# The low parts of the second layer's input on GpSimd, and two weight splits in other places

## The chip, the cores and the metric

One core of one Trainium2 chip runs the whole kernel. The metric is the device time of one execution in microseconds (us); the kernel before took 276.52 us, the median of three runs from 276.19 to 276.76. Engines: PE (TensorE, with weight loads shown apart as PEld), DVE (VectorE), ACT (ScalarE), POOL (GpSimd), and SP, which issues the DMAs.

## The reference, cut to what matters

One step of a decoder with two layers, on 256 prompt rows and 8 sample rows (264 columns in the kernel, which keeps features on partitions). Layer 0 is a gated short convolution, layer 1 block-sparse attention:

```python
xp = layernorm(DN_ALPHA * xp + yp, ln_g[0], ln_b[0])   # end of layer 0
q, k, v, z = jnp.split(x @ w_in_attn, 4, axis=-1)      # layer 1: 32 slabs of 128 columns
```

All arithmetic is float32.

## The kernel before, in words

To multiply in float32 precision, every operand is split into a rounded high part and a low part that is the rest (low = value - high), and a product is three matmuls: high x high, low x high, high x low. Weights come in 80 slabs of 128 output columns (1024 rows, so 128 x 1024 elements in a tile). For each slab n, `load(n)` issues the DMA of `raw`, `hi(n)` rounds it on ACT (L124), `lo(n)` subtracts on DVE (L129), and `mm` sends 24 matmuls to PE (L136 to L138), 8 blocks of the contraction times three. Here "split" means `lo(n)`.

The engines' queues are written out by hand: nothing reorders them. The order comes from hooks: `at(n, phase, f, ...)` puts work into slab n, and `begin(n)` runs the phases in the order dma, pe, s0, hi, lo, s1a, s1b, s1, s1c, then hi3 and lo3, ahead of the slab's matmuls. The tables `hi_slot` and `lo_slot` say at which slab the rounding and the split of a later slab stand. The load of the slab that takes over the `raw` buffer (there are four) stands behind the split.

Slabs 40 to 47 are the q part of layer 1's input projection. The normalised input x1 isn't ready when slab 40 is due, so slabs 40 to 46 (`i < NU`) multiply the not yet normalised rows (`m0`), and the evacuation repairs it: `u_evac` copies two columns (L580), then combines acc in PSUM with the norm's rows `nr` (L582) and multiplies (L583), on DVE; `u_fin` finishes on ACT (L586), and POOL copies the sample columns to `qs` (L587). Beside this, for each of 8 blocks m, x1 itself is made:

- `x1_norm(m)`: two DVE instructions on xf (L839, L840), from `nr`;
- `x1_affine(m)`: ACT scales and shifts (L844) and rounds to the high part `m1h` (L845);
- `x1_low(m)`: DVE subtracts to the low part `m1l` (L848).

Slab 47 is the first to multiply x1. It also has in its middle, between blocks 3 and 4, the 64 matmuls of the sample rows' scores (L745), which read `zq`, filled on DVE (L736) from `qs`. PSUM has three `acc` buffers in rotation: slab 47 takes the one of slab 44, which `u_evac` of slab 44 must have read.

Of the kernel before, what the change touches and what calls it, by code (L numbers as in the profile page):

```python
# [10 lines left out]
F32 = mybir.dt.float32  # L11
# [4 lines left out]
ALU = mybir.AluOpType  # L16
# [5 lines left out]
N = T + B  # L22
# [27 lines left out]
def build(tc, a):  # L50
    nc = tc.nc
    pe, act, dve, pool, sp = nc.tensor, nc.scalar, nc.vector, nc.gpsimd, nc.sync

    with ExitStack() as top:
# [35 lines left out]
        xf = cp.tile([128, NB, N], F32, name="xf")  # L90
# [40 lines left out]
        def mm(acc, n, mv, ks, first=True, last=True):  # L131
            mh, ml = mv
            w = acc.shape[-1]
            for k in ks:
                wh, wl = his[n][:, k, :], los[n][:, k, :]
                pe.matmul(acc, wh, mh[:, k, 0:w], start=first and k == ks[0], stop=False)  # L136
                pe.matmul(acc, wl, mh[:, k, 0:w], start=False, stop=False)  # L137
                pe.matmul(acc, wh, ml[:, k, 0:w], start=False, stop=last and k == ks[-1])  # L138
# [4 lines left out]
        def at(n, phase, f, *args):  # L143
            hooks.setdefault((n, phase), []).append(lambda: f(*args))

        def run(n, phase):
            for f in hooks.pop((n, phase), []):
# [2 lines left out]
        hi_slot = {4: 3, 5: 3, 6: 3, 7: 4, 8: 4, 9: 5, 10: 5, 11: 6, 38: 33, 39: 34, 40: 22, 41: 24, 42: 26,  # L150
                   43: 36, 44: 37, 45: 40, 46: 41, 47: 43, 48: 45, 49: 46, 50: 47, 51: 48, 52: 48, 53: 49,
                   54: 51, 55: 52, 56: 53, 57: 53, 58: 54, 65: 61, 66: 62, 67: 63, 68: 63, 78: 74}
        lo_slot = {4: 3, 5: 3, 6: 3, 7: 4, 8: 5, 9: 5, 45: 40, 46: 42, 47: 44, 51: 49, 52: 49,
                   53: 50, 54: 51, 55: 52, 56: 53, 57: 54, 58: 54, 61: 58, 62: 59, 63: 60, 64: 61, 65: 61, 66: 62, 67: 63, 39: 34}

        order = []
# [4 lines left out]
        for i, n in enumerate(order):  # L161
            hs = hi_slot.get(n, n - 5)
            late = "3" if 45 <= n < 50 else ""
            at(hs, "hi" + late, hi, n)
            ls = lo_slot.get(n, hs + 1)
            if n in (61, 62, 65):
                late = "4"
            elif ls in (56, 57, 58):
                late = "3"
            elif n == 46:  # L170
                late = ""
            at(ls, "lo" + late, lo, n)
            if i + 4 < len(order):
                at(ls, "lo" + late, load, order[i + 4])
# [360 lines left out]
        with tc.tile_pool(name="l1", bufs=1) as p1, ExitStack() as late_pool:  # L535
            x1 = pair[1]
# [305 lines left out]
            def x1_affine(m):  # L842
                c = xf[:, m]
                act.activation(c, c, AF.Identity, bias=ln.bcol(m), scale=ln.gcol(m))  # L844
                act.copy(x1[0][:, m, 0:N], c)  # L845

            def x1_low(m):
                dve.tensor_sub(x1[1][:, m, 0:N], xf[:, m], x1[0].bitcast(F32)[:, m, 0:N])  # L848

            S = 40  # L850

# [34 lines left out]
            for h in range(8):  # L886
                n = S + 16 + h
# [155 lines left out]
            split_late(41)  # L1043
            for m in (0, 1):
                x1_affine(m)
            mm(ac2[1], 41, pair[0], range(3, 7), first=False, last=False)
            for i in range(2):
                mm(ac2[i], 40 + i, pair[0], range(7, 8), first=False)
                at(42, "s0", u_evac, i, ac2[i])
                at(42, "s1", u_fin, i)  # L1050
            for n, norm, low in ((42, (2, 3), ()), (43, (4, 5), (0, 1)), (44, (6, 7), ()),
                                 (45, (), (2, 3)), (46, (), (4, 5, 6, 7))):
                for m in norm:
                    at(n, "s1", x1_norm, m)
                    at(n, "s1", x1_affine, m)
                for m in low:
                    at(n, "s1", x1_low, m)
            for i in range(2, 32):
                n = S + i
# [159 lines left out]
```

## Time and profile before

| what | value |
|---|---|
| median of 3 runs | 276.52 us (276.19 to 276.76) |
| the profiled execution | 276.77 us, of which the profile's span 275.0 us |
| busy | PE 98%, DVE 74%, ACT 62%, POOL 24% of the span |
| granted clock of PE | 1.00 |
| chain that ended last | PE 98% |

The span goes from the first to the last instruction; 1.8 us of the execution lie outside of it. A row of the order of time gives start, duration, engine, line, operation, output and inputs with shape; idle time of the engine ahead of it and what ended it stand in brackets. Matmuls overlap, so the distance of their starts tells more than their durations, and on the other engines, too, an instruction can start shortly before the last one has ended.

### The profile page before, as it was taken

The numbers are of one execution on the slowest core, as the hardware profiler recorded it, in microseconds if no ns is written. First come the engines' busy times: TensorE is split into PE (matmuls) and PEld (weight loads), VectorE is DVE, ScalarE is ACT, GpSimd is POOL, SyncE is SP. The second block draws the span as 40 slices with busy tenths as digits, with TensorE's granted clock in tenths as the row PEclk, the third lists the DMA queues.
The fourth block names the chain that finished last, engine by engine and source line by source line (L and its number), as shares of the span: only waits on it lengthen the run. The fifth ranks groups of instructions, "written<-read, shape, count | busy, mean of one in ns | idle before, by whom it ended". The sixth has DMA issues, their size and how long they took to land.

```text
span 275.0 us, 6282 instructions
## 1 busy us (share of the span) xinstructions
PE 270.2 (98%) x2307; PEld 254.7 (93%) x2307; DVE 203.5 (74%) x415; ACT 170.6 (62%) x348; POOL 64.9 (24%) x129
## 2 busy tenths in 40 slices
PE   8999999999999999999999999999999999999994
PEld 5999999999999999999999997999959996998883
DVE  3888966655775857979999839799857484994745
ACT  4786554453655628549686665888746854599302
POOL 1121532020110101961312365721100030000122
PEclk9999999999999999999999999999999999999999
DMA  7976879999785875142223999997989955782012
GB/s 245 401 274 223 281 286 333 396 360 377 245 266 197 283 227 189 56 147 76 80 76 99 343 401 357 337 393 233 354 308 348 391 183 174 219 272 75 1 76 88
DMA packets 24336, 66.48 MB, mean 242 GB/s; under 512 B 3058, under 2 KB 6898, under 8 KB 24178
## 3 DMA queue, kind: packets, MB, share of 16 engines
q1 hardware_dynamic: 23874, 65.69, 68.0%
q8 instruction: 18, 0.29, 0.4%
q10 hardware_dynamic: 432, 0.39, 0.4%
q14 instruction: 12, 0.10, 0.1%
HBM read 61.67 MB, written 3.35 MB: 236 GB/s over the span
## 4 chain that ended last, share of the span: by engine, by line
PE 98%; ACT 0%; DVE 0%; issue 0%
PE acc L136 24%; PE acc L137 24%; PE acc L138 24%; PE c L1010 4%; PE acc L472 3%; PE sd L745 3%; PE dps L796 3%; PE c1b L1010 2%; PE acc L1010 2%; PE acc L475 1%; PE so L1123 1%; PE warmp L80 1%; PE s L679 1%; PE o L717 1%; PE pt L707 1%; PE s L677 1%
## 5 line engine op out<-in xcount | busy, mean ns | idle before, releaser
L124 ACT CAST hi<-raw 128x1024 fp32r<-128x1024 f32 x76 | 79.0, 1049 | 34.3 <-DMA raw<-w 15.7
L129 DVE TENSOR_TENSOR lo<-raw,hi 128x1024 fp32r<-128x1024 f32 x76 | 92.7, 1230 | 7.1 <-ACT hi L124 3.9
L136 PE MATMUL acc<-m0h,hi 128*128 128x264 f32 (+1 forms) x280 | 79.4, 283 | 0.0
L138 PE MATMUL acc<-m0l,hi 128*128 128x264 f32 (+1 forms) x280 | 79.2, 283 | 0.0
L137 PE MATMUL acc<-m0h,lo 128*128 128x264 f32 (+1 forms) x280 | 79.2, 283 | 0.0
L136 PE MATMUL acc<-m1h,hi 128*128 128x264 f32 x264 | 76.4, 289 | 0.0
L138 PE MATMUL acc<-m1l,hi 128*128 128x264 f32 x264 | 74.6, 282 | 0.0
L137 PE MATMUL acc<-m1h,lo 128*128 128x264 f32 x264 | 74.5, 282 | 0.0
L137 PEld LDWEIGHTS acc<-m0h,lo 128*128 128x128 f32 x280 | 52.8, 189 | 0.0
L136 PEld LDWEIGHTS acc<-m0h,hi 128*128 128x128 f32 x280 | 52.6, 188 | 0.1
L138 PEld LDWEIGHTS acc<-m0l,hi 128*128 128x128 f32 x280 | 52.7, 188 | 0.0
L136 PEld LDWEIGHTS acc<-m1h,hi 128*128 128x128 f32 x264 | 49.6, 188 | 1.7 <-issue 0.8
L137 PEld LDWEIGHTS acc<-m1h,lo 128*128 128x128 f32 x264 | 49.8, 189 | 0.0
L138 PEld LDWEIGHTS acc<-m1l,hi 128*128 128x128 f32 x264 | 49.5, 188 | 0.0
L428 POOL COPY uo<-up 128x10 f32<-128x10 f32 x8 | 9.0, 1122 | 64.3 <-DVE up L427 58.5
L635 POOL COPY vs<-vh 128x8 f32<-128x8 f32 x8 | 3.0, 375 | 33.1 <-ACT vh L634 33.1
L688 DVE CUSTOM_DVE_ANT_0 P<-s,cst 128x128 f32<-128x128 f32 (+1 forms) x16 | 5.1, 355 | 6.2 <-PE s L679 6.2
L436 DVE SCALAR_TENSOR_TENSOR t<-up,cst,t 128x256 f32<-128x256 f32 x8 | 3.9, 483 | 6.9 <-ACT t L435 6.9
L825 POOL COPY zs<-z 128x8 f32<-128x8 f32 x8 | 3.0, 378 | 24.4 <-ACT z L824 24.4
L824 ACT ACTIVATE z<-acc 128x264 f32<-128x264 f32 x8 | 3.1, 386 | 9.0 <-PE acc L138 9.0
L952 ACT ACTIVATE zq<-raw 128x1024 f32<-128x1024 f32 x8 | 8.5, 1061 | 0.1
L427 DVE TENSOR_TENSOR up<-acc,h 128x264 f32<-128x264 f32 x8 | 3.4, 430 | 6.9 <-PE acc L138 6.9
(226 smaller groups left out, 446.5 us busy)
## 6 DMA issues: line engine op xcount, KB each, us to landing
raw<-w SPq DMA_DIRECT2D x76, 512.0 KB, 4.5
kv<-kc SPq DMA_DIRECT2D x32, 256.0 KB, 6.2
kv<-vc SPq DMA_DIRECT2D x16, 512.0 KB, 6.4
first<-first SPq DMA_DIRECT2D x6, 388.0 KB, 7.1
v_o<-vh SPq DMA_DIRECT2D x8, 132.0 KB, 5.5
xf<-kall SPq DMA_DIRECT2D x16, 64.0 KB, 2.6
kall<-gb SPq DMA_DIRECT2D x1, 1024.0 KB, 6.1
k_o<-kall SPq DMA_DIRECT2D x6, 132.0 KB, 5.4
```

Of the source, the lines that this page charges most:

```text
L124: act.copy(his[n][sl], raws[n][sl])
L129: dve.tensor_sub(los[n][sl], raws[n][sl], his[n].bitcast(F32)[sl])
L136: pe.matmul(acc, wh, mh[:, k, 0:w], start=first and k == ks[0], stop=False)
L137: pe.matmul(acc, wl, mh[:, k, 0:w], start=False, stop=False)
L138: pe.matmul(acc, wh, ml[:, k, 0:w], start=False, stop=last and k == ks[-1])
L428: pool.tensor_copy(uo[:, f], up[:, T:N + 2])
L472: pe.matmul(accs[s], wh, (mh, ml)[c], start=k == 0 and c == 0, stop=False)
L688: dve.tensor_tensor_reduce(out=P[sl], in0=s_ps[h][sl], in1=mask[sl], scale=-SCALE, scalar=3e38, op0=ALU.add, op1=ALU.min, accum_out=mx[:, ...
L745: pe.matmul(s[32 * j:32 * j + 16, 0:256], zq[:, o:o + 16], kt, start=step == 0 and i == 0, stop=step == 3 and i == 3)
L796: pe.matmul(dps[0][32 * j:32 * j + 32, 512 * c:512 * c + 512], pm[b2][pg][:, j, :], kv_tiles[step, j][:, 512 * c:512 * c + 512], start=ste ...
L952: act.activation(od, wide(raws, k), AF.Copy, accum_out=wsum[:, k:k + 1])
L1010: pe.matmul(acc, g[m][:, k, t], wide(d, k)[:, c0:c1], start=k == 0 and i == 0, stop=k == 7 and i == 2)
```

## The change

Three things are moved. All eight `x1_low` go from DVE to POOL, each pair behind its `x1_affine`. The splits of slabs 45 and 46 each stand one place later on DVE, behind evacuations. And the affines of blocks 6 and 7 stand behind `u_fin` of slab 43 on ACT.

```diff
-        lo_slot = {... 45: 40, 46: 42, 47: 44, ...}
+        lo_slot = {... 45: 42, 46: 43, 47: 44, ...}
...
-            elif n == 46:
+            elif n in (45, 46):
                 late = ""
...
             def x1_low(m):
-                dve.tensor_sub(x1[1][:, m, 0:N], xf[:, m], x1[0].bitcast(F32)[:, m, 0:N])
+                pool.tensor_tensor(x1[1][:, m, 0:N], xf[:, m], x1[0].bitcast(F32)[:, m, 0:N], ALU.subtract)
...
             for m in (0, 1):
                 x1_affine(m)
+                x1_low(m)
...
-            for n, norm, low in ((42, (2, 3), ()), (43, (4, 5), (0, 1)), (44, (6, 7), ()),
-                                 (45, (), (2, 3)), (46, (), (4, 5, 6, 7))):
+            for n, norm, low in ((42, (2, 3), ()), (43, (4, 5), (2, 3)), (44, (6, 7), (4, 5)),
+                                 (45, (), (6, 7))):
                 for m in norm:
                     at(n, "s1", x1_norm, m)
-                    at(n, "s1", x1_affine, m)
+                    at(n, "s1c" if n == 44 else "s1", x1_affine, m)
```

On POOL, from the copies of `nr` to the copy of `qs` of the fourth slab (q3); `zq`, `pr` and `pm` are cleared there. Before:

```order
L357 COPY nr_1903<-st0_1896 32x132 x4
L587 COPY qs_1862<-q0_1853 128x8
L587 COPY qs_1862<-q1_1854 128x8
L566 MEMSET zq_2027 128x1160
...
L587 COPY qs_1862<-q2_1855 128x8
L587 COPY qs_1862<-q3_1856 128x8
```

After:

```order
L357 COPY nr_1903<-st0_1896 32x132 x4
L848 TENSOR_TENSOR m1l_92<-xf_87,m1h_91 128x264 x2
L587 COPY qs_1862<-q0_1853 128x8
L587 COPY qs_1862<-q1_1854 128x8
L566 MEMSET zq_2025 128x1160
...
L848 TENSOR_TENSOR m1l_92<-xf_87,m1h_91 128x264 x2
L587 COPY qs_1862<-q2_1855 128x8
L848 TENSOR_TENSOR m1l_92<-xf_87,m1h_91 128x264 x2
L587 COPY qs_1862<-q3_1856 128x8
```

Low parts 4 and 5 now stand behind the copy of q2, and the copy of q3 behind them.

On DVE, from slab 41's evacuation (acc_1873) over slab 42's (t2_2038 before, t2_2036 after) to the norms that follow. Before:

```order
L583 TENSOR_TENSOR t2_1979<-t2_1979,nr_1903 128x264
L129 TENSOR_TENSOR lo46_1982<-raw46_1620,hi46_1948 128x1024
L839 TENSOR_TENSOR xf_87<-xf_87,nr_1903 128x264
...
L583 TENSOR_TENSOR t2_2038<-t2_2038,nr_1903 128x264
...
L848 TENSOR_TENSOR m1l_92<-xf_87,m1h_91 128x264 x2
L580 COPY uv_2086<-acc_2061 128x2
```

After:

```order
L583 TENSOR_TENSOR t2_1977<-t2_1977,nr_1903 128x264
L129 TENSOR_TENSOR lo45_1980<-raw45_1616,hi45_1913 128x1024
L839 TENSOR_TENSOR xf_87<-xf_87,nr_1903 128x264
...
L583 TENSOR_TENSOR t2_2036<-t2_2036,nr_1903 128x264
L129 TENSOR_TENSOR lo46_2039<-raw46_1620,hi46_1944 128x1024
...
L580 COPY uv_2088<-acc_2063 128x2
```

Split 45, which stood ahead of the first norms, takes the place of split 46; split 46 stands behind slab 42's evacuation, and the low parts are gone from ahead of slab 43's evacuation (L580).

On DVE, from slab 47's split over slab 44's evacuation to the filling of `zq`. Before:

```order
L129 TENSOR_TENSOR lo47_2103<-raw47_1743,hi47_2059 128x1024
L580 COPY uv_2132<-acc_2107 128x2
L582 SCALAR_TENSOR_TENSOR t2_2134<-nr_1903,uv_2132,acc_2107 128x264
L583 TENSOR_TENSOR t2_2134<-t2_2134,nr_1903 128x264
L848 TENSOR_TENSOR m1l_92<-xf_87,m1h_91 128x264 x2
L622 STREAM_SHUFFLE qsr_2168<-qs_1862 32x32
```

After:

```order
L129 TENSOR_TENSOR lo47_2107<-raw47_1743,hi47_2061 128x1024
L580 COPY uv_2136<-acc_2111 128x2
L582 SCALAR_TENSOR_TENSOR t2_2138<-nr_1903,uv_2136,acc_2111 128x264
L583 TENSOR_TENSOR t2_2138<-t2_2138,nr_1903 128x264
L622 STREAM_SHUFFLE qsr_2172<-qs_1862 32x32
```

The order of split and evacuation is the same; two low parts are gone behind them.

More of the change, by code (lines that the diff above doesn't have):

```diff
@@ L152, in build @@
                    54: 51, 55: 52, 56: 53, 57: 53, 58: 54, 65: 61, 66: 62, 67: 63, 68: 63, 78: 74}
-        lo_slot = {4: 3, 5: 3, 6: 3, 7: 4, 8: 5, 9: 5, 45: 40, 46: 42, 47: 44, 51: 49, 52: 49,
+        lo_slot = {4: 3, 5: 3, 6: 3, 7: 4, 8: 5, 9: 5, 45: 42, 46: 43, 47: 44, 51: 49, 52: 49,
                    53: 50, 54: 51, 55: 52, 56: 53, 57: 54, 58: 54, 61: 58, 62: 59, 63: 60, 64: 61, 65: 61, 66: 62, 67: 63, 39: 34}
```

## The prediction

> **What bounds the kernel now.** I read the page first (busy shares, chain), then PE's own waits, then the order of time on PE, DVE, ACT and POOL between 114 and 150 us, where the change lies.
>
> ```profile
> span 275.0 us, 6282 instructions
> PE 270.2 (98%) x2307; PEld 254.7 (93%) x2307; DVE 203.5 (74%) x415; ACT 170.6 (62%) x348; POOL 64.9 (24%) x129
> ...
> PE 98%; ACT 0%; DVE 0%; issue 0%
> ...
> raw<-w SPq DMA_DIRECT2D x76, 512.0 KB, 4.5
> ```
>
> The chain is PE nearly throughout. All idle time of PE that the trace puts down to somebody:
>
> ```profile
> PE warmp L80 <- PEq L1200: 0.8, 1, 0.8
> PE st L1139 <- ACT zq L1136: 0.5, 1, 0.5
> PE sd L745 <- issue: 0.2, 1, 0.2
> ```
>
> Only the last line, 0.2 us, lies where the change is. So the change can win hardly anything directly: work taken off DVE shortens the time only if PE waits for DVE. It can lose, if something that PE needs comes late. Where is that closest? At the start of slab 47, the first that reads x1 (columns: start us, us, engine, line):
>
> ```profile
> 142.11 0.28 PE L136 MATMUL acc<-m1h,hi 128*128 128x264 f32 x1
> ...
> 143.43 0.28 PE L138 MATMUL acc<-m1l,hi 128*128 128x264 f32 x1
> 143.86 0.50 PE L745 MATMUL sd<-kv,zq 128*16 128x256 f32 x2 [0.16 <-issue]
> ```
>
> The same stretch on DVE, before:
>
> ```profile
> 127.09 0.43 DVE L839 TENSOR_TENSOR xf<-xf,nr 128x264 f32<-128x264 f32 x1
> 127.56 0.44 DVE L840 TENSOR_TENSOR xf<-xf,nr 128x264 f32<-128x264 f32 x1
> ...
> 128.72 0.15 DVE L580 COPY uv<-acc 128x2 f32<-128x2 f32 x1
> ...
> 129.43 0.43 DVE L583 TENSOR_TENSOR t<-t,nr 128x264 f32<-128x264 f32 x1
> ...
> 130.84 1.22 DVE L129 TENSOR_TENSOR lo<-raw,hi 128x1024 fp32r<-128x1024 f32 x1
> 131.98 0.42 DVE L839 TENSOR_TENSOR xf<-xf,nr 128x264 f32<-128x264 f32 x1
> ...
> 134.38 0.43 DVE L583 TENSOR_TENSOR t<-t,nr 128x264 f32<-128x264 f32 x1
> 134.73 0.43 DVE L839 TENSOR_TENSOR xf<-xf,nr 128x264 f32<-128x264 f32 x1
> ...
> 136.35 0.77 DVE L848 TENSOR_TENSOR m1l<-xf,m1h 128x264 fp32r<-128x264 f32 x2
> 137.04 0.15 DVE L580 COPY uv<-acc 128x2 f32<-128x2 f32 x1
> ...
> 139.82 1.22 DVE L129 TENSOR_TENSOR lo<-raw,hi 128x1024 fp32r<-128x1024 f32 x1
> 140.96 0.15 DVE L580 COPY uv<-acc 128x2 f32<-128x2 f32 x1
> 141.15 0.49 DVE L582 SCALAR_TENSOR_TENSOR t<-nr,uv,acc 128x264 f32<-128x264 f32 x1
> ...
> 143.47 0.27 DVE L736 COPY zq<-qs 128x16 f32<-128x16 f32 x2
> ```
>
> DVE runs back to back. There are three acc buffers, so slab 47 writes into slab 44's, which L582 reads until 141.15 + 0.49 = 141.64. From a DVE end to the matmul that it frees takes 0.12 us (zq ends at 143.47 + 0.27 = 143.74, L745 starts at 143.86). PE could have started slab 47 at 141.76 and did at 142.11: **the spare is 0.35 us**. Whatever makes DVE later than that there, PE loses, and nothing gives it back, since PE has no idle time after it that could shrink.
>
> **Part 1: order and work of DVE.** What the norms wait for ahead of 127.09, on ACT:
>
> ```profile
> 124.78 2.17 ACT L357 COPY nr<-st 32x132 f32<-32x132 f32 x7
> ```
>
> A split (lo) costs DVE 131.98 - 130.84 = 1.14 us; two low parts 137.04 - 136.35 = 0.69. Before, slab 45's split ran ahead of 127.09, where DVE would otherwise have waited for ACT's copies of nr. Those end at 124.78 + 2.17 = 126.95; with the split gone the norms start at about 127.03, 0.06 earlier. Between there and 141.64 stand now both splits (45 takes 46's place, 46 comes behind the next evacuation: +1.14) and two low parts less (-0.69). Together -0.06 + 1.14 - 0.69 = +0.39. Against the spare of 0.35 that alone is 0.04 us of stall.
>
> **Part 2: eight low parts on POOL.** No row shows this operation there. The nearest is POOL's addition of the same shape, also with two SBUF inputs:
>
> ```profile
> 114.58 1.61 POOL L328 TENSOR_TENSOR sr<-sr,xf 128x264 f32<-128x264 f32 x1 [0.55 <-DVE xf L300]
> 116.15 0.95 POOL L329 TENSOR_TENSOR q<-q,sqm 128x264 f32<-128x264 f32 x1
> ...
> 120.50 0.76 POOL L329 TENSOR_TENSOR q<-q,sqm 128x264 f32<-128x264 f32 x1
> ```
>
> 0.76 us alone, 0.95 to 1.61 beside these rows of DVE:
>
> ```profile
> 114.36 1.21 DVE L129 TENSOR_TENSOR lo<-raw,hi 128x1024 fp32r<-128x1024 f32 x1
> 115.49 0.99 DVE L510 SCALAR_TENSOR_TENSOR m0l<-xf,cst,m0h 128x264 fp32r<-128x264 f32 x1
> 116.40 0.42 DVE L313 SCALAR_TENSOR_TENSOR xf<-ln,xf 128x264 f32<-128x264 f32 x1
> ```
> ```profile
> L510 DVE SCALAR_TENSOR_TENSOR m0l<-xf,cst,m0h 128x264 fp32r<-128x264 f32 x2 | 0.9, 488 | 0.0
> ```
>
> These exclude each other. POOL's row of 114.58 ends at 116.19, 0.62 after the split beside it (115.57): it worked only from 0.14 before the split's end. L510, 0.49 alone, then took 0.99 and ended at 116.48, 0.29 after POOL: it worked only from 0.20 before POOL's end. L313, with one input from PSUM, took its 0.42 in the middle of POOL's row: unhindered. So DVE's rows with two SBUF inputs (L129, L583, L839, L840) exclude a low part on POOL; L580 and L582, which read acc in PSUM, don't. In a dense row of DVE, the next instruction would start 0.08 before the last one's end e (114.36 + 1.21 - 115.49); with POOL in between it starts at e - 0.14 + 0.76 - 0.20 = e + 0.42. **A low part on POOL costs DVE up to 0.50 us, against 0.345 on DVE itself**, and nothing where it falls beside L580 and L582 or idle time: bounds 0 and 0.50 each. Which it is follows from when each rounding (m1h, L845) is out on ACT:
>
> ```profile
> 128.67 0.41 ACT L845 CAST m1h<-xf 128x264 fp32r<-128x264 f32 x1
> ...
> 129.63 0.41 ACT L845 CAST m1h<-xf 128x264 fp32r<-128x264 f32 x1
> ...
> 133.55 0.41 ACT L845 CAST m1h<-xf 128x264 fp32r<-128x264 f32 x1
> ...
> 134.50 0.41 ACT L845 CAST m1h<-xf 128x264 fp32r<-128x264 f32 x1
> ...
> 137.57 0.51 ACT L586 ACTIVATE q<-t,uv 128x264 f32<-128x264 f32 x1
> ...
> 145.31 1.98 ACT L124 CAST hi<-raw 128x1024 fp32r<-128x1024 f32 x2
> ```
>
> POOL follows ACT by 0.07 us (L586 above ends at 138.08):
>
> ```profile
> 138.15 0.19 POOL L587 COPY qs<-q 128x8 f32<-128x8 f32 x1 [4.30 <-ACT q L586]
> ```
>
> - Low 0: rounding out at 129.08, so on POOL from 129.15. L583 of the first evacuation, due at 129.37, starts at 129.15 + 0.76 - 0.20 = 129.71: 0.34.
> - Low 1: rounding out at 130.04, on POOL until 130.87, beside L580 and L582 of the second evacuation: 0.
> - Low 2: everything is 0.34 - 0.06 = 0.28 later by now. Rounding out at 133.96 + 0.28, on POOL from 134.31; L583, due at 134.66, starts at 134.87: 0.21.
> - Low 3: rounding out at 134.91 + 0.28 = 135.2, just as slab 46's split begins. It runs behind the split and pushes the next L839: 0.50.
> - Lows 4 and 5 stand in POOL's queue behind the copy of qs, which waits for L586, which stands behind the affines on ACT. These are 0.28 + 0.21 + 1.14 + 0.50 = 2.13 later now, so L586 ends at 140.2. Low 4 then gets in between the last L839 and its L840. Such an L840 would start 0.04 behind its L839 (127.09 + 0.43, 127.56), and now 0.42: 0.38. Low 5 follows at once, ahead of slab 47's split: 0.50.
>
> Sum of waits: 0.34 + 0.21 + 0.50 + 0.38 + 0.50 = 1.93. With part 1, L582 ends 2.32 late, at 143.96, and slab 47 starts at 144.08 instead of 142.11: **stall 2.0 us**.
>
> By the Trainium skill (SBUF — State Buffer, section "Who interferes with whom") a DVE instruction with two SBUF inputs contends with a GpSimd instruction that reads SBUF, and the second to issue is blocked until the first has finished. The trace agrees in kind; by the word of the rule DVE would wait to the full end of POOL's row, 0.20 longer than L510 did, and the estimate with five such waits would be 3.0 us of stall instead of 2.0.
>
> **Covered parts.** Lows 6 and 7 are needed in slab 47's second half, behind the 64 L745, whose time hides them:
>
> ```profile
> L745 PE MATMUL sd<-kv,zq 128*16 128x256 f32 x64 | 4.0, 379 | 0.2 <-issue 0.2
> ```
>
> Without that cover they would be a few tenths late, as they end near 145. Splits 45 and 46 end near 130.84 + 1.22 + 0.28 = 132.3 and, begun at 135.2, 136.4; their slabs start two and one slab ahead of 47, and a slab is 24 matmuls of (143.43 - 142.11) / 11 = 0.12 us, 2.9: at 136.3 and 139.2. That hides 46 by 2.7 us. On SP the loads of slabs 49 and 50 wait for those splits and start some 4 to 5 us later; nothing of SP stands behind them in that time that is due, and with 4.5 us to land they arrive by 141, ahead of the roundings of 49 and 50 at 145.31. The affines of 6 and 7 move behind one L586 on ACT: only lows 6 and 7 follow. The zq copies lose four low parts ahead of them (-1.39) but inherit the waits, so they end near 145.4 for L745 due 0.2 behind 144.08 + 143.43 - 142.11 = 145.4: the 0.2 us that PE waited there before may go or stay. I take 0.
>
> Sum: +2.0 on the profiled execution's 276.77, so 278.8; that run was 0.25 above the median, which gives **278.5** against 276.52.
>
> **Rivals.**
> - Not slower: POOL's low parts fall beside PSUM readers or cost DVE nothing, as beside L313. Then part 1 alone stands, 0.0 to 0.2 of stall, and the 0.2 at L745 may go: 276.3 to 276.7. It decides if the waits sum to under 0.5 us (0.55 for 0.2% less the 0.04). Against it: L510 twice its length. For it: L313.
> - Half: POOL's queue meets only two or three dense places, because DVE's next instruction gets in first. Stall 0.4 to 1.4: 276.9 to 277.9.
> - More: every one of the six low parts ahead of 47 costs the full 0.50, or DVE waits for POOL's full row: 6 x 0.50 + 0.04 = 3.0, 279.5. Against it: the 0.20 by which L510 worked ahead of POOL's end, and low 1's place.
>
> **How the numbers follow.** This measurement tells about 0.2% (0.55 us) from no change. Forecast (stall 1.4 to 2.6, so 277.9 to 279.1): 0.62. More: 0.06. Half: 0.14, of which 0.04 ends within 0.2%. Not slower: 0.18, nearly all of it no change; 0.04 for faster, since only 0.2 us of PE's waits are there to win. Slower 0.62 + 0.06 + 0.10 = 0.78, same 0.18, faster 0.04. The range takes in the half case and most of the not slower one, and leaves out the far end of "more": 276.5 to 279.2.
>
> **What would show it.** Right: a PE gap of about 2 us right ahead of the first L136 on m1h, put down to DVE; L839, L840, L583 and L129 at up to 0.9 or 1.7 us there; POOL's L848 at 0.76 to 1.6; L582 of slab 44 ending near 144. Wrong: no PE gap there, or one at slabs 45, 46 or L745 instead; L848 on POOL of quite another length than 0.76; DVE rows unstretched beside it.

## The result, and the profile after

| | before | after |
|---|---|---|
| median of 6 runs each | 276.36 us (276.08 to 276.76) | 278.76 us (278.51 to 279.11) |
| the profiled execution, its span | 276.77 us, 275.0 us | 279.11 us, 277.0 us |
| granted clock of PE | 1.00 | 1.00 |

The ratio is 1.0087 [1.0074, 1.0100]: 2.4 us slower. The page after, busy shares and chain:

```profile
span 277.0 us, 6287 instructions
PE 270.2 (98%) x2307; PEld 254.2 (92%) x2307; DVE 203.2 (73%) x407; ACT 170.4 (62%) x348; POOL 70.5 (25%) x137
...
PE 87%; DVE 7%; DMA 2%; ACT 2%; issue 1%; SPq 0%; DVEq 0%
```

PE's busy time is the same 270.2 us. DVE has eight instructions fewer, and yet its busy time is nearly the same: 203.2 instead of 203.5, where 8 x 0.345 = 2.8 us had been taken off. It has also come into the chain, 7% instead of 0%. PE's own waits (us in total, times, longest):

```profile
PE acc L136 <- DVE t L582: 1.9, 2, 1.7
...
PE acc L472 <- ACT m0h L215: 0.3, 1, 0.3
```

The first line is new: PE waits twice for `u_evac` to have read an acc buffer. The last is elsewhere, ahead of the stretch read below: the page before doesn't list it, and the kernels of the experiments show 0.2 us there or nothing. The order of time on PE shows the two places:

```profile
122.61 0.39 PE L136 MATMUL acc<-m0h,hi 128*128 128x266 f32 x1
...
138.85 0.28 PE L138 MATMUL acc<-m0l,hi 128*128 128x266 f32 x1
139.41 0.36 PE L136 MATMUL acc<-m0h,hi 128*128 128x266 f32 x1 [0.27 <-DVE t L582]
...
142.29 0.28 PE L138 MATMUL acc<-m0l,hi 128*128 128x266 f32 x1
144.23 0.36 PE L136 MATMUL acc<-m1h,hi 128*128 128x264 f32 x1 [1.66 <-DVE t L582]
...
145.62 0.28 PE L138 MATMUL acc<-m1l,hi 128*128 128x264 f32 x1
145.83 4.04 PE L745 MATMUL sd<-kv,zq 128*16 128x256 f32 x64
149.80 0.39 PE L136 MATMUL acc<-m1h,hi 128*128 128x264 f32 x1
```

The same places before (slab 47's first matmul, at 142.11, is shown above):

```profile
122.80 0.39 PE L136 MATMUL acc<-m0h,hi 128*128 128x266 f32 x1
...
139.05 0.28 PE L138 MATMUL acc<-m0l,hi 128*128 128x266 f32 x1
139.17 0.28 PE L136 MATMUL acc<-m0h,hi 128*128 128x266 f32 x1
...
141.98 0.28 PE L138 MATMUL acc<-m0l,hi 128*128 128x266 f32 x1
...
147.79 0.39 PE L136 MATMUL acc<-m1h,hi 128*128 128x264 f32 x1
```

The stretch, from the middle of slab 40 to behind L745, took 147.79 - 122.80 = 24.99 us before and takes 149.80 - 122.61 = 27.19 after: **2.20 us more**. From start to start, slab 46 begins 0.56 behind its predecessor's last matmul instead of 0.12 (+0.44), slab 47 1.94 instead of 0.13 (+1.81); the matmul behind each wait is some 0.07 slower to start, and ahead of L745 the distance is 0.21 instead of 0.43 (-0.22). After L745 the two programs stay the same distance apart to the end. The spans differ by 2.0, since after's stretch happened to begin 0.19 earlier; 2.1 instead of 1.8 us lie outside of the span. That last difference holds from run to run: 2.0 to 2.1 us lie outside in each of after's six runs, 1.9 to 2.1 with the low parts alone, and 1.7 to 1.9 in every other kernel here. So about 0.2 of the 2.4 us isn't in the stretch, and the runs don't show what sets it.

Why L582 is late stands on DVE and POOL:

```profile
129.19 0.83 DVE L583 TENSOR_TENSOR t<-t,nr 128x264 f32<-128x264 f32 x1
...
130.65 0.46 DVE L583 TENSOR_TENSOR t<-t,nr 128x264 f32<-128x264 f32 x1
...
134.56 0.71 DVE L583 TENSOR_TENSOR t<-t,nr 128x264 f32<-128x264 f32 x1
135.20 1.21 DVE L129 TENSOR_TENSOR lo<-raw,hi 128x1024 fp32r<-128x1024 f32 x1
136.33 0.98 DVE L839 TENSOR_TENSOR xf<-xf,nr 128x264 f32<-128x264 f32 x1
...
138.77 0.49 DVE L582 SCALAR_TENSOR_TENSOR t<-nr,uv,acc 128x264 f32<-128x264 f32 x1
...
140.92 0.88 DVE L840 TENSOR_TENSOR xf<-xf,nr 128x264 f32<-128x264 f32 x1
141.72 1.77 DVE L129 TENSOR_TENSOR lo<-raw,hi 128x1024 fp32r<-128x1024 f32 x1
...
143.59 0.49 DVE L582 SCALAR_TENSOR_TENSOR t<-nr,uv,acc 128x264 f32<-128x264 f32 x1
...
144.69 0.51 DVE L623 TENSOR_SCALAR qs<-qs,cst 32x32 f32<-32x32 f32 x1
```
```profile
134.23 0.75 POOL L848 TENSOR_TENSOR m1l<-xf,m1h 128x264 fp32r<-128x264 f32 x1 [0.20 <-ACT m1h L845]
135.18 1.85 POOL L848 TENSOR_TENSOR m1l<-xf,m1h 128x264 fp32r<-128x264 f32 x1 [0.20 <-ACT m1h L845]
...
140.55 1.86 POOL L848 TENSOR_TENSOR m1l<-xf,m1h 128x264 fp32r<-128x264 f32 x2
```

In the stretch up to slab 44's L582, every row of DVE that is longer than its usual 0.43 (L583, L839, L840) or 1.22 (L129) has a low part on POOL beside it, and every L582, which reads acc, keeps its 0.49. The excesses, low part by low part, are 0.40, 0.03, 0.28, 0.55, 0.45, 0.55 us: 2.26 in all. POOL waits in its turn: low 3, 0.75 long where it is alone, is 1.85 long behind slab 46's split.

### The profile page after: what moved, and what is told of

Same layout as the page of the kernel before. It is cut to its first block, busy times and chain, and to the rows that moved or that the text cites. A ratio compares the mean times of both kernels' runs of the same rounds, so it can differ in the third digit from the quotient of the medians.

```text
span 277.0 us, 6287 instructions
## 1 busy us (share of the span) xinstructions
PE 270.2 (98%) x2307; PEld 254.2 (92%) x2307; DVE 203.2 (73%) x407; ACT 170.4 (62%) x348; POOL 70.5 (25%) x137
## 4 chain that ended last, share of the span: by engine, by line
PE 87%; DVE 7%; DMA 2%; ACT 2%; issue 1%; SPq 0%; DVEq 0%
PE acc L136 21%; PE acc L138 21%; PE acc L137 21%; PE c L1010 4%; PE sd L745 3%; PE dps L796 3%; PE acc L472 2%; DMA first<-first 2%; PE c1b L1010 2%; PE acc L1010 2%; DVE lo L129 1%; PE so L1124 1%; DVE xf L839 1%; PE acc L475 1%; PE s L679 1%; PE o L717 1%
## 5 line engine op out<-in xcount | busy, mean ns | idle before, releaser
L129 DVE TENSOR_TENSOR lo<-raw,hi 128x1024 fp32r<-128x1024 f32 x76 | 93.2, 1236 | 7.0 <-ACT hi L124 6.6
L136 PE MATMUL acc<-m0h,hi 128*128 128x264 f32 (+1 forms) x280 | 79.4, 284 | 0.3 <-DVE t L582 0.3
L136 PE MATMUL acc<-m1h,hi 128*128 128x264 f32 x264 | 76.5, 290 | 1.7 <-DVE t L582 1.7
L136 PEld LDWEIGHTS acc<-m0h,hi 128*128 128x128 f32 x280 | 52.6, 188 | 0.6 <-PE acc L138 0.5
L136 PEld LDWEIGHTS acc<-m1h,hi 128*128 128x128 f32 x264 | 49.6, 188 | 3.5 <-ACT m1h L845 1.8
L428 POOL COPY uo<-up 128x10 f32<-128x10 f32 x8 | 8.0, 1004 | 65.8 <-DVE up L427 58.6
L848 POOL TENSOR_TENSOR m1l<-xf,m1h 128x264 fp32r<-128x264 f32 x8 | 7.7, 968 | 3.9 <-ACT m1h L845 3.7
```

Source lines behind the costliest of these rows:

```text
L129: dve.tensor_sub(los[n][sl], raws[n][sl], his[n].bitcast(F32)[sl])
L428: pool.tensor_copy(uo[:, f], up[:, T:N + 2])
L848: pool.tensor_tensor(x1[1][:, m, 0:N], xf[:, m], x1[0].bitcast(F32)[:, m, 0:N], ALU.subtract)
```

## The experiments

My theory is called "exclusion" in the expectations: the low parts on POOL and DVE's rows with two SBUF inputs shut each other out, and together with the splits that come later this makes slab 44's L582 late. Its rivals: "order", the moved splits alone make the loss; POOL's presence or the order of its queue, and not what it reads, makes it; and a low part costs more on POOL than on DVE wherever it stands. "Drift" below is how much later PE starts the same matmuls than before, from the middle of slab 40 to behind L745, read as above (after: +2.20).

**Only the low parts on POOL.** The splits stay where they were.

```diff
-                dve.tensor_sub(x1[1][:, m, 0:N], xf[:, m], x1[0].bitcast(F32)[:, m, 0:N])
+                pool.tensor_tensor(x1[1][:, m, 0:N], xf[:, m], x1[0].bitcast(F32)[:, m, 0:N], ALU.subtract)
...
(places of the low parts and affines as in the changed kernel; lo_slot as before)
```

> The kernel before, with all eight low parts on POOL and the affines placed as in the changed kernel, but the splits of slabs 45 and 46 where they were. Theory 'exclusion' (low parts on POOL and DVE instructions with two SBUF inputs shut each other out, about 0.5 us for each low part that meets a dense place): by the same walk as in the prediction, waits of 0.3 to 0.4 at the first evacuation and 0.4 to 0.5 at three more places, less 0.69 for the two low parts taken off DVE, less the spare of 0.35: PE stalls 0.6 to 1.0 us at slab 47, none at slab 46; about 277.1. Rival 'order' (the loss is the split that now stands ahead of slab 47; POOL costs nothing): no stall, and the 0.2 us wait at L745 goes: 276.2.

277.34 us (277.10 to 277.63) against 276.50: 1.0034 [1.0021, 1.0048], drift +0.90. Its waits of PE and its rows of DVE:

```profile
PE acc L136 <- DVE t L582: 0.9, 1, 0.9
```
```profile
128.62 0.83 DVE L583 TENSOR_TENSOR t<-t,nr 128x264 f32<-128x264 f32 x1
...
134.00 0.70 DVE L583 TENSOR_TENSOR t<-t,nr 128x264 f32<-128x264 f32 x1
...
135.08 0.87 DVE L840 TENSOR_TENSOR xf<-xf,nr 128x264 f32<-128x264 f32 x1
...
139.89 1.77 DVE L129 TENSOR_TENSOR lo<-raw,hi 128x1024 fp32r<-128x1024 f32 x1
```

There is one wait of PE, at slab 47. The same excesses appear without any split moved (0.40, 0.27, 0.44 and 0.55 in these rows; 0.03 for low 1 and 0.45 for an L840 not shown), so the moved splits don't cause them. Their sum of 2.14, less two low parts on DVE (0.69) and the spare (0.35), is 1.10; slab 47 starts 1.24 behind its predecessor's last matmul instead of 0.13, 1.11 more. That is a little over the 0.6 to 1.0 expected. The affines' new place is part of this kernel and wasn't run alone, but the excesses leave 0.01 for it.

**Only the splits moved.** The low parts stay on DVE.

```diff
-        lo_slot = {... 45: 40, 46: 42, 47: 44, ...}
+        lo_slot = {... 45: 42, 46: 43, 47: 44, ...}
...
-            elif n == 46:
+            elif n in (45, 46):
```

> The kernel before, with only the splits of slabs 45 and 46 moved as in the changed kernel; low parts stay on DVE. Theory 'exclusion': DVE is -0.06 + 1.14 = 1.08 us late at slab 44's evacuation, spare 0.35, so PE stalls 0.7 to 0.8 at slab 47, and L745 waits 0.4 more since zq is 1.1 late there and not only 0.7: 277.3 to 277.6, so more than the low parts alone, and DVE rows unstretched. Rival 'order': the whole 2.4 us of the changed kernel, 278.8.

277.48 us (277.21 to 277.65): 1.0036 [1.0021, 1.0052], drift +1.09. "Order" falls, as it asked for the whole loss; the splits make about half of it. PE and DVE:

```profile
141.60 0.28 PE L138 MATMUL acc<-m0l,hi 128*128 128x266 f32 x1
142.49 0.36 PE L136 MATMUL acc<-m1h,hi 128*128 128x264 f32 x1 [0.61 <-ACT q L586]
```
```profile
140.53 1.22 DVE L129 TENSOR_TENSOR lo<-raw,hi 128x1024 fp32r<-128x1024 f32 x1
...
141.86 0.49 DVE L582 SCALAR_TENSOR_TENSOR t<-nr,uv,acc 128x264 f32<-128x264 f32 x1
```

No row of DVE is stretched. One split of 1.14 between the norms' start (0.06 earlier) and L582, less the spare of 0.35, is 0.73; the distance ahead of slab 47 is 142.49 - 141.60 = 0.89, which is 0.76 more than the 0.13 before. Another 0.2 is L745 (0.4 was expected), whose `zq` is filled behind the same late rows. The wait at slab 47 is put down to ACT's L586, but L582 ends at 142.35, the usual 0.14 ahead: of several releasers the page names one, and DVE's was as late.

The two parts alone cost 0.90 and 1.09 and together 2.20. Ahead of slabs 46 and 47 the two alone add up to 0.38 less than both together (1.11 and 0.76 against 2.25), because each part alone can use up the spare of 0.35, and both together can use it once. L745 takes about 0.2 of that back: its distance changes by -0.23 and +0.23 in the two alone, and by -0.22 with both.

**POOL writes instead of computing.** In the changed kernel each low part is replaced by two memsets of its target, behind a copy of one column that keeps the wait for the rounding. The low parts of x1 are left out of this computation.

```diff
-                pool.tensor_tensor(x1[1][:, m, 0:N], xf[:, m], x1[0].bitcast(F32)[:, m, 0:N], ALU.subtract)
+                pool.tensor_copy(tiny[:, m:m + 1], x1[0].bitcast(F32)[:, m, 0:1])
+                for _ in range(2):
+                    pool.memset(x1[1].bitcast(F32)[:, m, 0:N], 0.0)
```

> The changed kernel, with each low part on POOL replaced by a copy of one column of m1h (it waits for the rounding as before) and two fills of m1l with zero: about the same time on POOL, but next to nothing read from SBUF. It leaves out the low parts of x1. Theory 'exclusion', as reads against second SBUF inputs: DVE rows unstretched (0.43 for L839, L840, L583, 1.22 for L129), stall at slab 47 0.0 to 0.2, the wait at L745 gone: 276.2 to 276.5. Rival 'POOL's mere presence or its queue order' (waits for the copies of qs, semaphores): as the changed kernel, 278.8. Rival 'order': 278.8 too.

276.88 us (276.20 to 277.52): 1.0016 [1.0004, 1.0027], drift -0.16. DVE's groups from 127 to 146 us (busy us, mean ns), first of the changed kernel, then of this one:

```profile
L129 DVE TENSOR_TENSOR lo<-raw,hi 128x1024 fp32r<-128x1024 f32 x3 | 4.2, 1397 | 0.0
...
L583 DVE TENSOR_TENSOR t<-t,nr 128x264 f32<-128x264 f32 x5 | 2.9, 573 | 0.2
```
```profile
L129 DVE TENSOR_TENSOR lo<-raw,hi 128x1024 fp32r<-128x1024 f32 x4 | 4.9, 1218 | 0.0
...
L583 DVE TENSOR_TENSOR t<-t,nr 128x264 f32<-128x264 f32 x6 | 2.6, 439 | 0.2
```

The stretching of DVE's two-input rows is gone but for 0.04 in one L583 (L736, a copy, is taken up in the last section), and so are PE's waits at slabs 46 and 47. POOL was busy at the same places for nearly the same time (a pair of memsets takes this):

```profile
134.90 1.02 POOL L850 COPY tiny<-m1h 128x1 f32<-128x1 f32 x1
135.86 0.69 POOL L852 MEMSET m1l<- 128x264 f32 x2
```

So what stretches DVE's two-input rows isn't POOL's presence or its queue, but that it reads SBUF. Even the copy of one column, 0.19 us elsewhere in this trace, took 1.02 beside slab 46's split. This agrees with the Trainium skill (SBUF — State Buffer, section "Who interferes with whom"): a DVE instruction with two SBUF inputs contends with a GpSimd instruction that reads SBUF, not with one that only writes it.

The time is still 0.4 above before, and above the range expected. It isn't lost in this stretch: PE's last matmuls come 0.18 earlier than before, as the chain's last PE line shows (before, then this kernel), but the span ends later.

```profile
271.25 0.40 PE st L1139 x2
```
```profile
271.07 0.40 PE st L1144 x2
```

From there to the span's end it is 275.0 - 271.25 = 3.75 us before and 275.2 - 271.07 = 4.13 here. Why, was not tested (more in the last section).

**Each low part twice.**

```diff
             def x1_low(m):
+                for _ in range(2):
-                pool.tensor_tensor(x1[1][:, m, 0:N], xf[:, m], x1[0].bitcast(F32)[:, m, 0:N], ALU.subtract)
+                    pool.tensor_tensor(x1[1][:, m, 0:N], xf[:, m], x1[0].bitcast(F32)[:, m, 0:N], ALU.subtract)
```

> The changed kernel, with each low part done twice on POOL (same result). Theory 'exclusion': the second one of each meets DVE as well, where the first one often had room; by the walk DVE is 1.9 us later still at slab 44's evacuation, L582 of slab 43 comes 2 us late for slab 46, slab 47 waits 1.8 more, and L745 waits up to 2 for zq: 280.5 to 282.5, with stretched rows of 0.8 to 1.0 (L839, L840, L583) and 1.8 (L129) about twice as many. Rivals 'order' and 'POOL's queue order': 278.8 to 279.3, since PE doesn't wait for the low parts themselves and only the copies of qs come later.

282.51 us (282.42 to 283.13): 1.0220 [1.0203, 1.0237], drift +6.26, 0.01 above the upper end of what was expected. PE waits at three places, ahead of slabs 46 and 47 and ahead of L745:

```profile
PE acc L136 <- DVE t L582: 4.1, 2, 2.4
PE sd L745 <- issue: 1.8, 1, 1.8
```
```profile
131.47 1.78 DVE L129 TENSOR_TENSOR lo<-raw,hi 128x1024 fp32r<-128x1024 f32 x1
...
138.00 0.98 DVE L839 TENSOR_TENSOR xf<-xf,nr 128x264 f32<-128x264 f32 x1
...
143.80 1.78 DVE L129 TENSOR_TENSOR lo<-raw,hi 128x1024 fp32r<-128x1024 f32 x1
```

```profile
142.64 4.62 POOL L849 TENSOR_TENSOR m1l<-xf,m1h 128x264 fp32r<-128x264 f32 x4
147.21 0.18 POOL L587 COPY qs<-q 128x8 f32<-128x8 f32 x1
```

No row is stretched by more than 0.56, but more rows are: nine up to slab 47's split, by 4.4 us, where after had six. Slab 45's split, 131.47 here, kept its usual 1.21 in after. So the price is per encounter, whatever POOL still has in its queue. The wait at L745 is in part of another kind: there POOL's queue itself is late, as the copy of qs comes behind four low parts, at 147.21. DVE stands idle for it for 0.78 us, and behind it L623, L624 and L736 (`zq`) are stretched in their turn, by 0.27, 0.55 and 0.47.

**Only low parts 0 and 1 on POOL.** The kernel before, with the first two low parts moved, which stand ahead of the dense place, and nothing else.

```diff
-                dve.tensor_sub(x1[1][:, m, 0:N], xf[:, m], x1[0].bitcast(F32)[:, m, 0:N])
+                (pool.tensor_tensor(x1[1][:, m, 0:N], xf[:, m], x1[0].bitcast(F32)[:, m, 0:N], ALU.subtract) if m < 2
+                 else dve.tensor_sub(x1[1][:, m, 0:N], xf[:, m], x1[0].bitcast(F32)[:, m, 0:N]))
...
             for m in (0, 1):
                 x1_affine(m)
+                x1_low(m)
...
-            for n, norm, low in ((42, (2, 3), ()), (43, (4, 5), (0, 1)), (44, (6, 7), ()),
+            for n, norm, low in ((42, (2, 3), ()), (43, (4, 5), ()), (44, (6, 7), ()),
```

> The kernel before, with only the low parts of blocks 0 and 1 on POOL, each right behind its rounding; all else as before. Theory 'exclusion': low part 0 meets L583 of the first evacuation and costs 0.40 as in the changed kernel, low part 1 falls beside L580 and L582, which read PSUM, and costs 0.03; 0.69 comes off DVE, so DVE is 0.2 to 0.3 us early from slab 43 on: no stall at slabs 46 and 47, and the wait of 0.2 us ahead of L745 shrinks to 0.1 or less: 276.2 to 276.5, which the times can hardly tell from before, but the traces can. Rival 'every low part on POOL costs more than on DVE': DVE 0.3 late, spare at slab 47 used up, L745 later: 276.6 to 276.9.

276.12 us (275.63 to 276.53) against 276.61: 0.9987 [0.9977, 0.9996], drift -0.10. DVE's row beside low 0, and PE around L745:

```profile
128.79 0.84 DVE L583 TENSOR_TENSOR t<-t,nr 128x264 f32<-128x264 f32 x1
```
```profile
142.79 0.28 PE L138 MATMUL acc<-m1l,hi 128*128 128x264 f32 x1
143.12 1.24 PE L745 MATMUL sd<-kv,zq 128*16 128x256 f32 x15
```

Two low parts less on DVE (-0.69) cost it 0.41 there and 0.03 beside low 1. The net 0.25 stands behind a spare at slab 47, where it brings nothing, and shortens the distance ahead of L745 from 0.43 to 0.33. Its median is the lowest of all kernels here, but of the medians' 0.49 us against before the traces show only 0.1 as coming from the edit. The rest isn't explained by it; from trace to trace, the stretch begins up to 0.8 us earlier or later (122.80 before, 121.99 with the low parts alone).

**Norms later.** The kernel of the experiment above, with the norms and affines of blocks 6 and 7 behind slab 44's evacuation, to get slab 47 and L745 free of every wait.

```diff
-            for n, norm, low in ((42, (2, 3), ()), (43, (4, 5), ()), (44, (6, 7), ()),
-                                 (45, (), (2, 3)), (46, (), (4, 5, 6, 7))):
+            for n, norm, low in ((42, (2, 3), ()), (43, (4, 5), ()), (44, (), ()),
+                                 (45, (), (2, 3)), (46, (6, 7), (4, 5, 6, 7))):
```

> As the one with two low parts on POOL, and the norms and affines of blocks 6 and 7 behind the filling of zq and slab 45's evacuation, in front of low parts 4 to 7. Theory 'exclusion' with DVE's queue as what PE waits for: what PE needs first (split 47, slab 44's evacuation, zq) comes 0.3 to 0.8 us earlier, bound by slab 47's rounding on ACT; no stall at slabs 46 and 47, no wait at L745: 0.2 us less than before, 276.2 to 276.3, and no more, since PE then waits for nothing there. Against it: low parts 6 and 7 become the last thing PE needs in slab 47 (blocks 6 and 7 at about 148.3, low parts ready at about 147.4); if they are late, PE stalls there and it comes out slower.

276.93 us (276.43 to 278.06) against 276.61: 1.0015 [1.0003, 1.0026]. A miss: the wait at L745 did go (drift -0.31), but 40 us later PE's weight loads have two new ones, which were not there before. The waits between 183 and 190 us:

```profile
PEld o L717 <- DVE m0l L663: 0.2, 1, 0.2
PEld pt L707 <- DVE m0l L663: 0.2, 1, 0.2
```

PE has lost 0.49 behind them. On DVE the splits of slabs 48 to 50 are some 1.4 us later, with them the loads that follow, and the softmax of the attention comes about 1 us later at that place. That this is the path from the one to the other is argued from the order of the rows and was not tested.

## Why the prediction was right

Forecast 278.5, measured 278.76, by the mechanism forecast: of the 2.4 us, 2.2 lie in the stretch that the forecast named, for its 2.0. The 0.2 outside of the span it did not hold. By its steps:

- **The spare of 0.35 at slab 47** decided the place: the main wait is ahead of the first L136 on m1h, put down to L582, as forecast. In after's times L582 ends at 143.59 + 0.49 = 144.08 and the matmul starts 0.15 later.
- **Part 1, the order.** The experiment on the splits alone gave 0.76 at slab 47 for the 0.73 that the same arithmetic gives without the low parts' -0.69.
- **Part 2, the waits.** Forecast 0.34, 0, 0.21, 0.50, 0.38, 0.50, sum 1.93; measured 0.40, 0.03, 0.28, 0.55, 0.45, 0.55, sum 2.26. The places are right, each of them; the size is 0.05 to 0.07 short in each of the five. That is nearly all one term: I took from L510 that DVE works again from 0.20 ahead of POOL's end. Here it is 0.14 to 0.15: low 3 ends at 135.18 + 1.85 = 137.03, and the L839 beside it ends at 137.31, 0.43 of work, so it began at 136.88. L510 was another operation with another length; for L839 and L129 a dense encounter costs 0.55, not 0.50.
- **The full end of POOL's row.** The Trainium skill (SBUF — State Buffer, section "Who interferes with whom") says that the blocked instruction waits until the other has finished, which would have given 3.0 us; DVE's start 0.14 ahead of POOL's recorded end decides against that size, and for the kind. Whether POOL stops reading before its record ends, the traces don't tell.
- **A gap that I didn't list.** I named a gap at slab 46 as a sign of being wrong, and there is one, of 0.44. My own walk held it: slab 43's L582 comes behind low parts 0 to 3 and split 46, and I worked only slab 44's. It changes nothing in the sum, since slab 47's start is set by DVE: without the first gap the second would be 2.25 instead of 1.81. But the sentence on what would show the forecast wrong was too strict.
- **The lengths listed as signs** were exceeded: L839 0.98 for 0.9, L129 1.77 for 1.7, and POOL's longest low part 1.85 for 1.6. The first two are the same short term. Low 3 came at the very start of slab 46's split and had to wait for nearly all of it; the row from which I took 1.6 had met only a part of one.
- **L745.** I left open whether its wait goes, and took 0; it went, -0.22. That made up for most of what the waits were short of, and this was luck: the sum held neither.
- **The covered parts** hold: PE waits for no split, no load and neither of low parts 6 and 7.

The rivals: "not slower" is refuted by the stretched rows; "half" by the experiment with the low parts alone, where five of six cost 0.27 to 0.55; "more" by low 1, which cost 0.03 beside L580 and L582.

## What to carry to other kernels

An operation moved from a busy engine to an idle one relieves the busy one less than it seems, or not at all, where the two contend for memory: here each subtraction taken off DVE saved 0.345 us and cost up to 0.55 when POOL read SBUF among DVE's two-input rows. Ask also where the saving and the cost stand. Over all eight low parts DVE came out even (203.5 and 203.2 us busy), but only two of them had stood ahead of slab 44's L582, for which PE waits, and six ran on POOL ahead of it: 0.69 us saved there against 2.26 lost. Low parts that run on POOL only behind that point were not tried. Look in the trace for a pair of rows of both engines that overlap, take from it who stretches whom, and then walk the stretch row by row, placing each moved operation by the time at which its input is out. Move only those that fall beside rows that don't contend (one input from PSUM, a pause), and check not only the slab that is nearest to a wait, but also the ones ahead of it.

## What the runs showed of the hardware that I had not expected

- L623, a TENSOR_SCALAR of 32x32 with one data input, took 0.51 us in after and 0.23 in the kernel with two low parts on POOL, where POOL reads nothing beside it. Low 7 ran beside it in after. The pair of copies of L736, with one SBUF input, took 0.74 instead of 0.27 beside the doubled low parts, and 0.43 in the kernel with memsets, beside a one-column copy and a memset. The same section of the Trainium skill counts `tensor_scalar` among the operations that can take the pair of ports that DVE shares with GpSimd, when their operands meet its conditions; L623's row agrees, and I had counted only rows with two inputs.
- POOL is shut out too, and for longer than DVE, even with its smallest reads: a copy of 128x1 went from 0.19 to 1.02 us beside a split, and a low part from 0.75 to 1.85.
- The stretch from PE's last matmuls to the span's end was 3.75 us before (POOL x129 instructions in all) and 4.13 us with the memsets (x153). With the doubled low parts it was 281.3 - 277.23 = 4.07 (x145), but in after 277.0 - 273.26 = 3.74 with x137, so it doesn't grow with each instruction. With the memsets it is lost behind DVE's last instruction, which ends 0.19 us earlier than before, so in the program's closing instructions: one of POOL's three drains there took 0.21 instead of 0.08 us, which is a part of it. What sets it stays open.
